# First projection's products recorded among the tokens' transposes

## The chip, the cores and the metric

The kernel runs on one core of one Trainium2 chip. The metric is the device time of one execution in microseconds; lower is better. The kernel before was run three times (1632.19, 1634.96 and 1637.48 us, median 1634.96). One further execution was recorded by the hardware profiler.

## The reference, cut to what matters

One layer of a hybrid decoder for 1024 prompt tokens and 32 sample tokens (8 sequences of 4). The part that the change touches is the first norm and the columns of the input projection that feed the state-space group:

```python
def token_mixer(h, ...):              # h = rms_norm(x, norm_g[0])
    z = h @ w_in                      # 1024 -> 512 (a) + 512 (g) + 512 (u)
    a, g, u = z[..., :512], z[..., 512:1024], z[..., 1024:]
    v = a * sigmoid(g)                # convolution group
    ...
    s, h_last = s5_layer(u, ...)      # 32 groups, 64 complex states each, scan over time
```

After that come a convolution of width 31, LayerNorm, the S5 scan, two output projections, cross-attention over 256 memory tokens, and a SwiGLU feed-forward network of width 2816. All of it is computed in fp32 accuracy.

## The kernel before

Tokens stand along the free dimension: 1056 tokens are two halves (b = 0, 1) of two parts (s) of 264 columns, 8 sample tokens and 256 prompt tokens. A feature tile is [128, 2, 264]. Every weight product is three fp32r matmuls: weight and activation are each split into a high part (ScalarE, `hi`) and a low part (VectorE or GpSimd, `lo`), and `mac` (L187) issues high x high, high x low, low x high, each for both parts s, so one feature tile of one output block costs 6 matmuls of 264 columns, and one output block of 128 columns costs 48.

The input stage loads the rows of half 0 (four DMAs of 512 KB, L126), transposes them on TensorE into 8 feature tiles (`tokens_in`, L280: per tile four 128x128 transposes and two of 8 columns), and has ScalarE copy each tile out of PSUM twice: `xf` (L290, which SyncE's queue stores to DRAM as the residual) and `hi` scaled by the norm's gain (L293). VectorE forms `lo` (L294). `tokens_rsqrt` makes the norm's factors r0 by a Newton iteration on VectorE and small matmuls with a matrix of ones. The norm's factor is applied after the product: `project_u` (L325) runs the 48 matmuls of one output block, multiplies by r0 (L81, tile `u`) and stores `u` to DRAM. Blocks j = 0, 1 are made here for both halves, from two weight tiles `wu` (L321, `st_wi`, `hi_wi`, `lo_wi`); the stage after it (`filler` and `s5_stream`) interleaves the convolution group's projections (`pg`, `pa`) with the S5 stream. That stream has 16 pairs of groups; for each two pairs `s5_matrices` has VectorE build tables (`ct`, `ebd`, `fbd`), TensorE turns them (`psS`, `psK`), `s5_states` multiplies them with `uf`, which is `u` read back from DRAM (`pw`), VectorE forms `X` and `Y`, scans (`M`), and `s5_outputs` gives `py`. In parallel with the input stage VectorE computes the S5 parameters in a long chain of operations on 16 columns, which starts from four small loads (`srow`, `ldt`, `drow`).

The order of instructions on each engine is fixed when the kernel is built: a list scheduler takes what is ready by its own timing, the highest priority first, and `high_priority(offset=...)` shifts a block's priority (a larger offset comes earlier). On the chip each engine then runs its list in order. PSUM tiles come from three pools: `mm` (two buffers), `pw` (one) and `sm` (two); `mm_tile` takes every third tile from `pw`, unless the list `streams` holds something.

[...]

Of the kernel before, what the change touches and what calls it, by code (L numbers as in the profile page):

```python
# [13 lines left out]
ALU = mybir.AluOpType  # L14
# [4 lines left out]
P = 128  # L19
D = 1024  # L20
KT = 8
NB = 8
W = 264
# [19 lines left out]
def decode_step(ctx: ExitStack, tc: tile.TileContext, I, O):  # L43
    nc = tc.nc
    act, dve, pool, pe, sync = nc.scalar, nc.vector, nc.gpsimd, nc.tensor, nc.sync
# [9 lines left out]
    def unit(name, dt=F32, shape=(P, 2, W), tag="act"):  # L55
        return acts.tile(list(shape), dt, tag=tag, bufs=BUFS[tag], name=name)

    def tmp(name, dt=F32, shape=(P, 2, W)):
        return unit(name, dt, shape, "tmp")
# [3 lines left out]
    def mm_tile(name):  # L63

        turn[0] += 1
        third = turn[0] % 3 == 0 and not streams
        return ps.tile([P, 2, 512], F32, tag="pw" if third else "mm", bufs=1 if third else 2, name=name)

    def pw_tile(name):
        return ps.tile([P, 2, 512], F32, tag="pw", bufs=1, name=name)  # L70

    streams = []

    def sm_tile(name):
        return ps.tile([P, 512], F32, tag="sm", bufs=2, name=name)

    def dscr(name, shape):
        return dram.tile(shape, F32, tag=name, name=name)

    def tt(out, a, b, op, eng=None):  # L80
        (eng or dve).tensor_tensor(out, a, b, op)  # L81
# [18 lines left out]
    def run(*gens):  # L100

        gens = [g for g in gens if g is not None]
        while gens:
            gens = [g for g in gens if next(g, END) is not END]

    END = object()
# [14 lines left out]
    def load_rows(b):  # L121
        rows.append([[startp.tile([P, D], F32, name=f"rows{b}{s}{i}") for i in range(2)] for s in range(2)])
        with tc.high_priority(offset=4000000 - 2000000 * b):
            for s in range(2):
                for i in range(2):
                    sync.dma_start(rows[b][s][i], xp[2 * b + s, i * P:(i + 1) * P])  # L126
# [57 lines left out]
    def wcols(w, n, name, eng=None):  # L184
        return wrect(w, 0, w.shape[1] // P, n * P, P, f"{name}{n}", eng)

    def mac(outs, whi, wlo, xhi, xlo, parts, first, last):  # L187

        for i, (a, b) in enumerate(((whi, xhi), (whi, xlo), (wlo, xhi))):
            for out, part in zip(outs, parts):  # L190
                pe.matmul(out, lhsT=a, rhs=part(b), start=first and i == 0, stop=last and i == 2)  # L191

    both = [lambda x: x[:, 0, :], lambda x: x[:, 1, :]]
    one = [lambda x: x]

    def dense(out, wh, wl, xs, first=True, last=True, k0=0, step=P):

        outs = [out[:, 0, :W], out[:, 1, :W]]
        for k, (xh, xl) in enumerate(xs):
            c = slice(k0 + k * step, k0 + k * step + P)  # L200
            mac(outs, wh[:, c], wl[:, c], xh, xl, both, first and k == 0, last and k == len(xs) - 1)
# [69 lines left out]
    h = [[None] * KT for _ in range(2)]  # L271
    r0 = [None, None]
# [7 lines left out]
    def tokens_in(b):  # L280
        for k in range(KT):
            c = slice(k * P, (k + 1) * P)
            pt = mm_tile(f"xt{b}{k}")
            for s in range(2):
                q = slice(32 * (2 * b + s), 32 * (2 * b + s) + 8)
                for i in range(2):
                    pe.transpose(pt[:, s, 8 + i * P:8 + (i + 1) * P], rows[b][s][i][:, c], ident)
                pe.transpose(pt[:, s, 0:8], srows[q, c], ident[q, q])
            xt = startp.tile([P, 2, W], F32, tag="xf", bufs=13, name=f"xf{b}{k}")
            act.activation(xt, pt[:, :, :W], AF.Copy)  # L290
            sync.dma_start(xres[b][k], xt)
            hi, lo = unit(f"h{b}{k}h", F32R), unit(f"h{b}{k}l", F32R)
            act.activation(hi, pt[:, :, :W], AF.Copy, scale=gain(0, k))  # L293
            dve.scalar_tensor_tensor(lo, xt, gain(0, k), hi.bitcast(F32), op0=ALU.mult, op1=ALU.subtract)  # L294
            h[b][k] = (hi, lo)
            yield

    def tokens_rsqrt(b):
        for s in range(2):
            for i in range(2):  # L300
                sum_squares(1 + 4 * b + 2 * s + i, rows[b][s][i])
        if b == 0:
            sum_squares(0, srows)
        n0, n1 = (0, 5) if b == 0 else (5, 9)
        newton(y0[:, n0:n1], ssq[:, n0:n1], D, 1e-6)
        r0[b] = rtile(f"x{b}")
        for s in range(2):
            q = slice(32 * (2 * b + s), 32 * (2 * b + s) + 8)
            o = sm_tile(f"r0{b}{s}")
            d8 = tiny.tile([104, 8], F32, tag="d8", name=f"d8{b}{s}")  # L310
            dve.tensor_scalar(d8[q], ident[q, q], y0[q, 0:1], None, op0=ALU.mult)
            pe.matmul(o[:, 0:8], lhsT=ones[q], rhs=d8[q], start=True, stop=True)
            for i in range(2):
                d = tiny.tile([P, P], F32, tag="rd", bufs=3, name=f"r0d{b}{s}{i}")
                j = 1 + 4 * b + 2 * s + i
                dve.tensor_scalar(d, ident, y0[:, j:j + 1], None, op0=ALU.mult)
                pe.matmul(o[:, 8 + i * P:8 + (i + 1) * P], lhsT=ones, rhs=d, start=True, stop=True)
            act.activation(r0[b][:, s, :], o[:, :W], AF.Copy)

    with tc.high_priority(offset=1500000):  # L320
        wu = {j: wcols(I["w_in"], 8 + j, "wi", dve if j == 0 else pool) for j in range(2)}  # L321
    load_rows(1)
    unat = [[dscr(f"u{b}_{j}", [P, 2, W]) for j in range(4)] for b in range(2)]

    def project_u(j, b, w):  # L325
        pu = mm_tile(f"pu{j}{b}")
        dense(pu, *w, h[b])
        u = tmp(f"u{j}{b}")
        tt(u, pu[:, :, :W], r0[b], ALU.mult)
        sync.dma_start(unat[b][j], u)  # L330
# [28 lines left out]
    def ahead(gen):  # L359

        while True:
            with tc.high_priority(offset=1000000):
                if next(gen, END) is END:
                    return
            yield
# [108 lines left out]
    tt(f_re, f_re, den, ALU.mult)  # L474
    tt(f_im, f_im, den, ALU.mult)
    gt = [ahead(tokens_in(b)) for b in range(2)]
    run(gt[0])
    tokens_rsqrt(0)
    for j, n in ((0, 2), (1, 3)):
        for _ in range(n):  # L480
            next(gt[1])
        project_u(j, 0, wu[j])
    pp = sm_tile("pp1")
    perm = unit("perm", F32, (4 * TAPS, 4, TAPS), "co")
    pool.memset(perm, 0.0)
# [47 lines left out]
        tt(bbar[:, o], bbar[:, o], b1, op, pool)  # L533

    run(gt[1])
    with tc.high_priority(offset=1000000):
        tokens_rsqrt(1)
    for j in range(2):
# [983 lines left out]
    for s4 in range(4):  # L1522
        b, s = s4 // 2, s4 % 2
# [44 lines left out]
```

## Time and profile before

| | |
|---|---|
| median of three runs | 1634.96 us |
| profiled execution's own time | 1629.99 us |
| its span, first to last instruction | 1628.3 us |
| TensorE busy / weight loads busy | 1501.8 us (92%) / 1454.1 us (89%) |
| VectorE, ScalarE, GpSimd busy | 1004.9 us (62%), 685.6 us (42%), 327.6 us (20%) |
| mean granted TensorE clock | 0.972 |

The table says what each engine did over the whole span. It doesn't say what set the end of the stage that is changed: that is read from the stage's own stretch of the timeline. The input stage ends where the first matmul of `pg` starts, at 69.78 us. A matmul's own duration includes its latency; the pace is the distance between starts.

### The profile page before, as it was taken

Reading aid. Unit: us, or ns where it says so; the run is one execution under the profiler, and the core shown is the slowest. Engines: PE = TensorE matmul, PEld = TensorE weight load, DVE = VectorE, ACT = ScalarE, POOL = GpSimd, SP = SyncE. Lnnn points to the kernel's source line nnn. Section 1 sums busy time; section 2 is a strip of 40 time slices with the busy share of each in tenths; the row PEclk is TensorE's granted clock in tenths of the full one; section 3 lists DMA queues with packets and bytes.
Section 4 is the critical chain, followed back from the end, with each engine's and each line's share of the span. In section 5 each row is a group of like instructions: output and inputs, shape, how many; then the busy total and the mean of one; then the engine's idle time right before and its main releaser. Section 6 shows DMA issues by size and latency. Waiting matters only on the chain. (4 is left out here: it accounts for less than half of the span.)

```text
span 1628.3 us, 29327 instructions
## 1 busy us (share of the span) xinstructions
PE 1501.8 (92%) x11731; PEld 1454.1 (89%) x11731; DVE 1004.9 (62%) x1689; ACT 685.6 (42%) x1242; POOL 327.6 (20%) x409
## 2 busy tenths in 40 slices
PE   7999889889999979878968899999999999999995
PEld 5888878889999979778968899999999999999995
DVE  6889786466468855484486877666555542444345
ACT  6444534457564544374355643333333334122122
POOL 1366566330334420051120000000000000000005
PEclk9998999999999989989989999999999999999998
DMA  8522223456244503454436643333222234232124
GB/s 232 166 73 70 65 71 101 139 155 202 78 138 152 184 14 117 143 168 140 142 118 182 218 141 124 124 119 99 80 79 79 67 113 149 89 101 69 50 66 158
DMA packets 216116, 194.33 MB, mean 119 GB/s; under 512 B 21900, under 2 KB 180036, under 8 KB 215972
## 3 DMA queue, kind: packets, MB, share of 16 engines
q1 hardware_dynamic: 215852, 192.30, 38.3%
q8 instruction: 92, 1.51, 0.4%
q14 instruction: 44, 0.36, 0.1%
q10 hardware_dynamic: 128, 0.16, 0.0%
HBM read 146.33 MB, written 46.51 MB: 118 GB/s over the span
## 5 line engine op out<-in xcount | busy, mean ns | idle before, releaser
L1497 POOL COPY ysam<-ya 128x8 f32<-128x8 f32 x32 | 5.6, 192 | 745.9 <-DVE ya L81 745.1
L81 DVE TENSOR_TENSOR ya<-ya,fd 128x528 f32<-128x528 f32 x64 | 45.1, 704 | 105.8 <-PE fd L191 105.8
L176 ACT ACTIVATE hi_wd<-st_wd 128x1024 fp32r<-128x1024 f32 x20 | 21.2, 1060 | 121.5 <-PE fd L191 121.3
L191 PE MATMUL pao<-oth,hi_wa 128*128 128x264 f32 x256 | 53.8, 292 | 14.4 <-ACT mg L979 13.3
L81 DVE TENSOR_TENSOR c<-c,X 128x528 f32<-128x528 f32 x51 | 35.9, 703 | 39.7 <-PE X L1310 39.7
L191 PEld LDWEIGHTS pao<-oth,hi_wa 128*128 128x128 f32 x256 | 40.9, 194 | 15.2 <-ACT mg L979 13.9
L191 PE MATMUL pao<-otl,hi_wa 128*128 128x264 f32 x256 | 53.7, 291 | 0.0
L191 PE MATMUL pao<-oth,lo_wa 128*128 128x264 f32 x256 | 53.2, 289 | 0.5 <-DVE lo_wa L84 0.5
L643 PE MATMUL pcv<-vf,cm 128*128 128x128 f32 x320 | 45.2, 292 | 7.2 <-ACT ob L645 4.5
L643 PEld LDWEIGHTS pcv<-vf,cm 128*128 128x128 f32 x320 | 41.9, 206 | 9.0 <-issue 5.7
L191 PEld LDWEIGHTS pao<-oth,lo_wa 128*128 128x128 f32 x256 | 40.8, 193 | 0.8 <-DVE lo_wa L84 0.7
L191 PEld LDWEIGHTS pao<-otl,hi_wa 128*128 128x128 f32 x256 | 41.0, 194 | 0.1
L84 DVE TENSOR_TENSOR lo_wa<-st_wa,hi_wa 128x1024 fp32r<-128x1024 f32 x16 | 19.4, 1214 | 34.0 <-ACT hi_wa L176 34.0
L84 DVE TENSOR_TENSOR kl<-pkr,kh 128x512 fp32r<-128x512 f32 x32 | 21.9, 690 | 28.7 <-ACT kh L89 28.5
L84 DVE TENSOR_TENSOR lo_wd<-st_wd,hi_wd 128x1024 fp32r<-128x1024 f32 x20 | 24.5, 1225 | 24.4 <-ACT hi_wd L176 21.2
L224 DVE RECIPROCAL r_n<-r_n 128x528 f32<-128x528 f32 x8 | 27.6, 3450 | 12.0 <-ACT r_n L223 12.0
L753 DVE TENSOR_TENSOR_SCAN M<-rho,X 128x256 f32<-128x256 f32 x32 | 29.8, 956 | 7.4 <-POOL X L81 7.3
L89 ACT ACTIVATE wc<-t 128x512 fp32r<-128x512 f32 x22 | 13.9, 632 | 47.2 <-PE X L1310 25.1
L89 ACT ACTIVATE kh<-pkr 128x512 fp32r<-128x512 f32 x32 | 18.9, 598 | 30.7 <-PE pkr L1135 29.5
L81 DVE TENSOR_TENSOR c<-c,c 128x528 f32<-128x528 f32 x45 | 31.6, 702 | 0.1
L645 ACT ACTIVATE ob<-pcv,cbias 128x128 f32<-128x128 f32 x32 | 11.6, 364 | 46.4 <-PE pcv L643 46.3
L1385 ACT ACTIVATE c<-Z 128x528 f32<-128x528 f32 x22 | 13.5, 612 | 41.4 <-PE Z L1310 41.4
(2047 smaller groups left out, 5720.1 us busy)
## 6 DMA issues: line engine op xcount, KB each, us to landing
hr<-hid SPq DMA_DIRECT2D x44, 264.0 KB
ww<-in_w_gate_dram SPq DMA_DIRECT2D x22, 512.0 KB
ww<-in_w_up_dram SPq DMA_DIRECT2D x22, 512.0 KB
st_wd<-in_w_down_dram SPq DMA_DIRECT2D x20, 512.0 KB
hid<-c SPq DMA_DIRECT2D x38, 264.0 KB
xo<-x SPq DMA_DIRECT2D x32, 264.0 KB
kr<-in_cache_mem_k_dram SPq DMA_DIRECT2D x32, 256.0 KB
st_wo<-in_w_out_dram SPq DMA_DIRECT2D x16, 512.0 KB
```

The costliest lines, as they stand in the source:

```text
L81: (eng or dve).tensor_tensor(out, a, b, op)
L84: eng.tensor_tensor(lo, x, hi.bitcast(F32), ALU.subtract)
L89: act.activation(hi, x, AF.Copy)
L176: act.activation(hi[:, :cols], stv, AF.Copy)
L191: pe.matmul(out, lhsT=a, rhs=part(b), start=first and i == 0, stop=last and i == 2)
L224: dve.reciprocal(r, r)
L643: pe.matmul(o, lhsT=cm[:, d].rearrange("p c t -> p (c t)"), rhs=vf[:, g, 4 - d:CH - d], start=d == 0, stop=d == 4)
L645: act.activation(ob[:, g4], o, AF.Identity, bias=cbias[:, gg:gg + 1])
L753: dve.tensor_tensor_scan(out=M[:, i], data0=rho[:, pair:pair + 1].to_broadcast([P, 256]), data1=X[:, i], initial=0.0, op0=ALU.mult, op1=AL ...
L1385: act.activation(c22, Z[:, :, :W], AF.Copy)
L1497: pool.tensor_copy(ysam[:, n, 2 * b + s, :], yacc[b][n][:, s, 0:8])
```

## The change

Three things change. The two weight tiles of the first projection get a higher priority, above the small parameter loads and the rows of half 1. A new generator `project_steps` records the first projection's products of half 0 one feature tile at a time, so that the 6 matmuls of tile k can stand between transposes; its PSUM tile comes from `pw`, and `streams` holds something until half 1 has been transposed, so that transposes have only the two `mm` buffers. Block j = 0 is recorded two tiles behind the transposes of half 0, block j = 1 among the transposes of half 1. Blocks of half 1 go through `project_u` as before.

```diff
-    with tc.high_priority(offset=1500000):
+    with tc.high_priority(offset=2500000):
         wu = {j: wcols(I["w_in"], 8 + j, "wi", dve if j == 0 else pool) for j in range(2)}
...
+    def project_steps(j, b, w):
+
+        pu = pw_tile(f"pu{j}{b}")
+        for k in range(KT):
+            c = slice(k * P, (k + 1) * P)
+            mac([pu[:, 0, :W], pu[:, 1, :W]], w[0][:, c], w[1][:, c], *h[b][k], both, k == 0, k == KT - 1)
+            yield
+        u = tmp(f"u{j}{b}")
+        tt(u, pu[:, :, :W], r0[b], ALU.mult)
+        sync.dma_start(unat[b][j], u)
...
     gt = [ahead(tokens_in(b)) for b in range(2)]
-    run(gt[0])
+    gu = [ahead(project_steps(j, 0, wu[j])) for j in range(2)]
+    streams.append(1)
+    for k in range(KT):
+        next(gt[0])
+        if k > 1:
+            next(gu[0])
+    next(gt[0], END)
     tokens_rsqrt(0)
-    for j, n in ((0, 2), (1, 3)):
-        for _ in range(n):
-            next(gt[1])
-        project_u(j, 0, wu[j])
+    run(gu[0])
+    for k in range(KT):
+        next(gt[1])
+        next(gu[1])
+    run(gu[1])
...
     run(gt[1])
+    streams.clear()
     with tc.high_priority(offset=1000000):
         tokens_rsqrt(1)
```

On SyncE's queue, at the program's start, the two weight tiles `st_wi` (512 KB each) and the small loads stand so before:

```order
L126 DMA rows_89<-in_x_prompt_dram 128x1024
L138 DMA ldt<-in_log_dt_dram 16x2
L135 DMA srow<-in_lam_im_dram 16x128
L133 DMA srow<-in_lam_re_dram 16x128
L141 DMA drow<-in_d_skip_dram 16x32
L126 DMA rows_148<-in_x_prompt_dram 128x1024
...
L126 DMA rows_151<-in_x_prompt_dram 128x1024
L173 DMA st_wi_136<-in_w_in_dram 128x8x128
L173 DMA st_wi_142<-in_w_in_dram 128x8x128
L334 DMA h0row<-in_state_ssm_re_dram 128x128
```

The weights stand at the end of this piece, just ahead of `h0row`. With the change the same piece of SyncE's queue reads:

```order
L126 DMA rows_89<-in_x_prompt_dram 128x1024
L173 DMA st_wi_136<-in_w_in_dram 128x8x128
L173 DMA st_wi_142<-in_w_in_dram 128x8x128
L135 DMA srow<-in_lam_im_dram 16x128
L138 DMA ldt<-in_log_dt_dram 16x2
L133 DMA srow<-in_lam_re_dram 16x128
L141 DMA drow<-in_d_skip_dram 16x32
L126 DMA rows_148<-in_x_prompt_dram 128x1024
...
L126 DMA rows_151<-in_x_prompt_dram 128x1024
L345 DMA h0row<-in_state_ssm_re_dram 128x128
```

The weights moved ahead of the four small loads and of half 1's rows (148 to 151); the rows of half 0 (86 to 89) stay first.

On TensorE, with the change, the list from the fourth transposed tile (`xt_385`) on begins so (`pq` are the transposes of the small loads, `pu_378` is block 0 of half 0); before, the tiles of half 0 stood here one behind the other and `pu` began ten tiles in:

```order
L384 MATMUL pq<-ident,srow 128x48
L385 MATMUL pq<-ident,drow 32x16
L191 MATMUL pu_378<-h00h,hi_wi_138 128x264 x2
L191 MATMUL pu_378<-h00l,hi_wi_138 128x264 x2
L191 MATMUL pu_378<-h00h,lo_wi_139 128x264 x2
L191 MATMUL pu_378<-h01h,hi_wi_138 128x264
L287 MATMUL xt_385<-ident,rows_86 128x128
L287 MATMUL xt_385<-ident,rows_87 128x128
L191 MATMUL pu_378<-h01h,hi_wi_138 128x264
L288 MATMUL xt_385<-ident,srows 128x8
```

What moved: after three tiles the products of tile k follow, and each further tile's transposes stand between them; `pq`, and with it the small loads, stands ahead of the first product.

On VectorE, around the multiplications `u_868` and `u_920` that close the projections of half 1, the list before is this (`ct_040` to `ct_051`, `ebd`, `fbd` are S5 tables of the first two pairs, `ct_140` of the next two, `lo_wi_971` a weight tile of the next stage):

```order
L81 TENSOR_TENSOR ebd_936<-ct_041_1033,ct_041_1034 64x2x4x16 x2
L84 TENSOR_TENSOR lo_wi_965<-st_wi_962,hi_wi_964 128x1024
...
L81 TENSOR_TENSOR ct_050_1039<-pw,cmat 128x160
...
L81 TENSOR_TENSOR fbd_937<-ct_050_1039,ct_050_1040 64x2x5x16 x2
...
L81 TENSOR_TENSOR fbd_937<-ct_051_1045,ct_051_1046 64x2x5x16 x2
L81 TENSOR_TENSOR ct_140_1255<-pwr,bbar 128x2x64
...
L84 TENSOR_TENSOR lo_wi_971<-st_wi_968,hi_wi_970 128x1024
...
L81 TENSOR_TENSOR u_868<-pu_819,r_x_796 128x528
L81 TENSOR_TENSOR u_920<-pu_871,r_x_796 128x528
L81 TENSOR_TENSOR ebd_936<-ct_140_1255,ct_140_1256 64x2x4x16 x2
```

Here all tables for the first two pairs, and `ct_140`, stand ahead of both `u`. With the change the same place on VectorE reads:

```order
L84 TENSOR_TENSOR lo_wi_965<-st_wi_962,hi_wi_964 128x1024
...
L84 TENSOR_TENSOR lo_wi_971<-st_wi_968,hi_wi_970 128x1024
L81 TENSOR_TENSOR ct_040_1028<-pwr,bbar 128x2x64
L81 TENSOR_TENSOR u_868<-pu_819,r_x_796 128x528
L81 TENSOR_TENSOR u_920<-pu_871,r_x_796 128x528
...
L81 TENSOR_TENSOR ebd_936<-ct_040_1027,ct_040_1028 64x2x4x16 x2
L81 TENSOR_TENSOR ct_041_1033<-pwr,bbar 128x2x64
...
L81 TENSOR_TENSOR ebd_936<-ct_041_1033,ct_041_1034 64x2x4x16 x2
L81 TENSOR_TENSOR ct_050_1039<-pw,cmat 128x160
...
L81 TENSOR_TENSOR fbd_937<-ct_050_1039,ct_050_1040 64x2x5x16 x2
```

The tables of the first two pairs, and the first of the next two, moved behind both `u`. From the S5 stream's sixth pair on (some 130 us into the span before) the lists of the two kernels are all but the same.

## Rows read from the trace of the kernel before

**Rows 1.** Stretches (us): span, busy by engine (instructions), granted clock, DMA share, GB/s.

```profile
13.66:28.20 14.54, 14.54 (x55) 9.32 (x55) 12.28 (x50) 10.49 (x18) 2.80 (x4) 1.00 1.01 281
...
31.40:63.80 32.40, 32.40 (x244) 29.50 (x243) 27.76 (x104) 15.28 (x29) 9.73 (x21) 1.00 0.67 208
63.80:69.78 5.98, 2.56 (x21) 1.61 (x19) 5.85 (x15) 3.75 (x9) 1.96 (x3) 0.96 0.38 111
69.78:72.60 2.82, 2.82 (x13) 2.82 (x14) 2.62 (x8) 1.37 (x5) 1.08 (x3) 0.50 0.79 241
...
79.24:108.77 29.53, 29.53 (x224) 28.04 (x224) 24.32 (x41) 13.44 (x24) 21.70 (x30) 1.00 0.19 56
```

**Rows 2.** TensorE's timeline: start, length, line, out<-in, count, idle before and its releaser.

```profile
10.35 0.90 PE L287 MATMUL xt<-ident,rows 128*128 128x128 f32 x3 [1.08 <-DMA rows<-in_x_prompt_dram]
...
28.80 0.64 PE L191 MATMUL pu<-h00l,hi_wi 128*128 128x264 f32 x2
29.24 0.64 PE L191 MATMUL pu<-h00h,lo_wi 128*128 128x264 f32 x2
...
37.44 0.41 PE L191 MATMUL pu<-h07l,hi_wi 128*128 128x264 f32 x2
37.69 0.40 PE L191 MATMUL pu<-h07h,lo_wi 128*128 128x264 f32 x2
...
43.11 0.38 PE L287 MATMUL xt<-ident,rows 128*128 128x128 f32 x2
...
44.10 0.39 PE L191 MATMUL pu<-h03h,lo_wi 128*128 128x264 f32 x1
...
69.78 0.81 PE L191 MATMUL pg<-h00h,hi_wi 128*128 128x264 f32 x2 [0.98 <-DVE u L81]
```

**Rows 3.** VectorE's timeline, the same columns.

```profile
10.69 0.22 DVE L370 COPY srow<-ldt 16x128 f32<-16x128 f32 x1 [4.30 <-DMA ldt<-in_log_dt_dram]
12.11 0.21 DVE L376 COPY lam<-pq 128x48 f32<-128x48 f32 x1 [1.20 <-PE pq L374]
...
22.81 1.23 DVE L84 TENSOR_TENSOR lo_wi<-st_wi,hi_wi 128x1024 fp32r<-128x1024 f32 x1 [2.07 <-ACT hi_wi L176]
...
28.11 0.50 DVE L404 TENSOR_SCALAR th<-th 128x16 f32<-128x16 f32 x1
...
30.18 0.76 DVE L294 SCALAR_TENSOR_TENSOR h07l<-xf,gains,h07h 128x528 fp32r<-128x528 f32 x1
...
57.36 0.28 DVE L81 TENSOR_TENSOR ebd<-ct,ct 64x128 f32<-64x128 f32 x1
...
67.27 0.49 DVE L81 TENSOR_TENSOR ct<-pwr,bbar 128x128 f32<-128x128 f32 x2
...
69.02 1.32 DVE L81 TENSOR_TENSOR u<-pu,r_x 128x528 f32<-128x528 f32 x2
```

**Rows 4.** ScalarE's timeline, the same columns.

```profile
21.72 1.06 ACT L176 ACTIVATE hi_wi<-st_wi 128x1024 fp32r<-128x1024 f32 x1 [3.43 <-DMA st_wi<-in_w_in_dram]
...
28.66 0.22 ACT L406 ACTIVATE ab<-th 128x16 f32<-128x16 f32 x1 [0.88 <-DVE th L404]
28.90 1.28 ACT L407 ACT_TABLE_LOAD   x1
...
30.58 0.60 ACT L290 ACTIVATE xf<-xt 128x528 f32<-128x528 f32 x1
31.07 0.70 ACT L293 ACTIVATE h10h<-xt,gains 128x528 fp32r<-128x528 f32 x1
```

**Rows 5.** VectorE's later timeline, the same columns.

```profile
72.72 1.10 DVE L81 TENSOR_TENSOR ct<-pw,cmat 128x160 f32<-128x160 f32 x2
...
75.82 0.49 DVE L81 TENSOR_TENSOR ct<-pwr,bbar 128x128 f32<-128x128 f32 x2
...
79.24 0.69 DVE L81 TENSOR_TENSOR X<-pw,tab 128x512 f32<-128x512 f32 x1 [1.25 <-ACT wsam L743]
...
108.77 2.30 DVE L753 TENSOR_TENSOR_SCAN M<-rho,X 128x256 f32<-128x256 f32 x2
```

## The prediction, made before the changed kernel was run

> **What bounds the kernel now.** I read the stretches first, then the timelines of the three engines in that stage. Over its whole span TensorE is 92% busy, but the input stage is not like the rest, and the stretches show three parts of it [rows 1]. From 13.66 to 28.20 TensorE is busy without a gap, with transposes; from 31.40 to 63.80 it is busy without a gap, with products; from 63.80 to 69.78 it is busy for 2.56 of 5.98 us while VectorE is busy for 5.85. So the stage is bound by TensorE first and by VectorE at its end: `pg`, which opens the next stage at 69.78, waits for `u` [rows 2], which VectorE made at 69.02 behind S5 tables [rows 3].
>
> The pace of TensorE is the second thing to see. Two products start 0.44 us apart at 28.80 and 0.25 us apart at 37.44 [rows 2]: 0.22 and 0.122 us each for 264 columns. The stretch from 69.78 to 72.60 has a granted clock of 0.50, which is 1.2 GHz. The column says 1.00 for 13.66 to 28.20, but since the products at 28.80 have the pace of 1.2 GHz I take that stretch for 1.2 GHz too: there 55 matmuls of transposes and factors took 14.54 us, 0.264 each, so a tile of six costs 1.59 us, against 0.99 for one between products (43.11 to 44.10) [rows 1, 2]. TensorE thus spent some 14 us on transposes at half pace, busy all the time, and the clock did not rise.
>
> **Part by part.** My sum goes along the new order, with durations of the profiled execution.
>
> *Loads.* The last rows of half 0 landed at 10.35 [rows 2]. The first weight tile was ready at 21.72 [rows 4], and between them 2 MB of rows and 1 MB of weights landed: 3.1 MB in 11.4 us, 0.27 MB per us. With the weights right behind half 0's rows, 1.05 MB takes 3.9 us: 14.2. The small loads now stand behind them: `ldt`, which VectorE got at 10.69 [rows 3], comes at about 14.5, 3.8 us later; at best it is not held up (10.7), at worst the queue delays it another 2 us. Half 1's rows then land by 22, and the order uses them only after six tiles of products, past 25, so they cost nothing. This is the price of the change: the S5 parameter chain starts 3.8 us late, and so does the first product, since `pq` stands ahead of it in TensorE's list. `lam` moves from 12.11 to 15.9, the first product to 15.5.
>
> *First projection.* TensorE has to run 48 products, 7 tiles and the factors' ten small matmuls: 48 x 0.122 + 7 x 0.99 + 1.3 = 14.1 us at full pace. `pg` ran 2.8 us slowly before the clock rose [rows 1], which costs 1.4: the block would end at 15.5 + 14.1 + 1.4 = 31.0. But the eighth tile is held by something else. ScalarE's list has `ab`, a table load and two sines ahead of it, and `ab` waits for VectorE's `th` [rows 4]. VectorE took 16.0 us from `lam` to `th` (12.11 to 28.11), of which 2.07 was a wait for weights that now come early, and 1.8 is work that now stands ahead of `lam`: the weight's low part, 1.1, and the first tile's, 0.7 like the eighth's [rows 3]. That leaves 12.1 us, so `th` comes at 28.0. Then `ab`, the table and the sines (2.1), the eighth tile's two copies (1.1) [rows 4], its low part (0.7) and four products (0.5): the block ends at 32.5. Before, it ended at 37.9 [rows 2]. Gain here 5.4 us, of which TensorE could have had 6.9. The small parameter tables (`wrow`, `prow`), whose transposes now stand near the block's end, have 0.5 MB less of stored tiles ahead of them; I cost them at nothing, up to 1.5 us.
>
> *The rest of the projections.* TensorE needed 25.8 us from there to the end of the last product at 63.8, without a gap [rows 1, 2]. The same work remains. Three tiles of half 1 now stand in a row with two PSUM buffers, where ScalarE needs 1.1 us for one against 0.99: with some waiting 1.2 us. It ends at 59.5, and `u` is made by 60.5. Can VectorE follow? The eighth low part was done by 30.9, and from 31.40 VectorE had 27.8 us of work to 63.80 and 5.2 more to 69.02 [rows 1, 3]. Nine rows of S5 tables, from 57.36 to 67.27, 7.4 us in all, go behind `u` [rows 3]. So 25.6 us from 32.0, where the eighth low part is done now: 57.6, about 2 us of slack. Both `u` end at 60.5 instead of 70.3: 9.8 us earlier. `pg` starts at about 59.5.
>
> *What is given back.* The tables did not vanish. Behind `u` VectorE now has the 7.4 us, and 3.4 more that stood there before and still has to come ahead of the first `X` (two tables, a `sg`, two small ones); the first `X` comes 10.8 us behind `u`, at 71.3. The other path to it, `u` stored and read back, took 9.0 us (70.3 to 79.24) and would give 69.5, so VectorE decides. Gain 7.9. From `X` to the scan of the fourth pair at 108.77 VectorE worked 24.3 us in 29.5 [rows 1, 5]. Five rows of tables, 72.72 to 75.82, 3.45 us [rows 5], now lie in this stretch. They can fill its 5.2 us of waiting wholly (27.8 us) or not at all (33.0), and one more activation table load, 1.28 us [rows 4], may fall on the chain. I take half of the waiting as filled: 30.4 us, the scan at 101.7, a gain of 7.1. Then the lists are the same, and all engines are shifted alike.
>
> Sum: 4.3 (the products end at 59.5, not 63.8) + 5.5 (`u` follows them after 1.0 us instead of 6.5) - 1.9 - 0.8 = 7.1 us. The profiled execution took 1629.99 and would take 1622.9. It lies 5 us under the median of the runs, 1634.96; I take the difference off that: **1628**.
>
> [...]
>
> **The rivals.**
>
> *The clock stays at 1.2 GHz through the first projection* (slower). The order puts 1.59 us of transposes beside each 1.32 us of products. For it: transposes alone did not raise the clock in 14 us [rows 1]. Against it: where tiles stood between products at 43.11 the pace stayed full [rows 2], though there the clock was already up. Price: 48 x 0.22 + 7 x 1.59 + 2.6 = 24.3, so the block ends at 39.8, later than before; three more tiles and the small transposes at half pace cost 2.8, and the clock rises only in block 1, for another 1.6. The products end at 71.2, `u` at 72.2, the first `X` 10.8 later at 83.0, which is 3.8 later than before, and the scan loses another 0.9: 4.7 us slower, 1640. It decides if products still start 0.44 us per two beyond some 25 us.
>
> *The S5 stream eats the gain.* The tables fill no waiting, the table load falls on the chain, and `X` is 1 us later: 33.0 + 1.3 from 72.3 puts the scan at 106.6, a gain of 2: 1633. For it: VectorE waited there for GpSimd and ScalarE in short pieces that a table of 0.5 to 1 us overfills. Against: the tables are independent work, and lie exactly between waits.
>
> *More than forecast.* The eighth tile is not held up by `th`, the read-back decides `X` (69.5 less 1.5), the tables fill all waiting: the scan at 68.0 + 27.8 = 95.8 to 2 us later, a gain of 11 to 13: 1623. For it: at 31.0 TensorE alone would allow it. Against: `lam` can hardly come earlier.
>
> **Chances.** Forecast (gain of 5 to 9) 0.45; eaten gain (0 to 5) 0.25; more 0.12; slow clock 0.18. A change of 0.3%, 4.9 us, is about what a measurement tells from none. Faster takes the forecast, the larger gain, and loses a little at the forecast's lower end: 0.55. The slow clock at 1640 lies on the bound, and two thirds of it count as slower: 0.12. The rest is 0.33. The range reaches from the larger gain (1622) to the slow clock (1640), each with 1 to 2 us for the scatter of the runs, 1632 to 1637 before: 1620 to 1641; the forecast's own is 1625 to 1631.
>
> **What would show it.** Right: `hi_wi` near 14 us, `lam` near 16; products 0.25 us per two before 25 us; block 0's last product near 32.5; `pg` near 59.5 with hardly a wait; the first `X` near 71, the fourth scan near 102. Wrong: products at 0.44 past 25 us, VectorE not ready for `u` at 60, `X` waiting for something other than VectorE, or a shift at the fourth scan that is gone by the end of the S5 stream.

## The result, and the profile after

The changed kernel takes 1646.34 us (median of 8 runs, 1639.07 to 1651.55); the kernel before, run beside it, took 1635.22 (median of 8, 1627.42 to 1638.61). The ratio is 1.0074, 95% interval 1.0049 to 1.0098: slower by 11 us, where 1628 was predicted and 1641 was the upper end of the range. The profiled execution took 1639.07, span 1637.4, and was the fastest of the eight; a second one further down lies near the median. One run below (1671.00 us, of the changed kernel with plain products) fell into a slower state and is left out of its median and ratio.

First the stretches of the changed kernel, with the columns of [rows 1]: the first projection at half pace, then from VectorE's eighth low part to `u`, from `u` to the first `X`, and on to the fourth pair's scan.

```profile
15.15:34.20 19.05, 19.05 (x76) 15.40 (x75) 14.79 (x75) 10.18 (x20) 3.81 (x7) 1.00 0.88 221
35.87:70.09 34.22, 34.22 (x258) 31.15 (x258) 28.44 (x97) 18.85 (x35) 12.99 (x23) 1.00 0.59 183
70.09:81.72 11.63, 10.65 (x82) 9.49 (x81) 10.70 (x28) 5.32 (x12) 3.75 (x5) 1.00 0.40 114
81.72:112.72 31.00, 27.29 (x186) 25.59 (x186) 29.41 (x51) 14.39 (x25) 19.90 (x29) 0.89 0.18 52
```

TensorE's timeline after, with the columns of [rows 2]:

```profile
15.15 0.81 PE L191 MATMUL pu<-h00h,hi_wi 128*128 128x264 f32 x2
15.76 0.64 PE L191 MATMUL pu<-h00l,hi_wi 128*128 128x264 f32 x2
16.20 0.64 PE L191 MATMUL pu<-h00h,lo_wi 128*128 128x264 f32 x2
...
31.38 0.64 PE L191 MATMUL pu<-h04h,lo_wi 128*128 128x264 f32 x2
31.82 0.42 PE L191 MATMUL pu<-h05h,hi_wi 128*128 128x264 f32 x1
...
34.49 0.40 PE L191 MATMUL pu<-h05h,lo_wi 128*128 128x264 f32 x2
34.73 0.28 PE L191 MATMUL pu<-h06h,hi_wi 128*128 128x264 f32 x1
...
38.78 0.41 PE L191 MATMUL pu<-h07h,lo_wi 128*128 128x264 f32 x2
...
66.11 0.40 PE L191 MATMUL pg<-h00h,hi_wi 128*128 128x264 f32 x2
```

The products start 13 us earlier than before, and then run at half pace for 19 us: 0.44 us for two at 15.76 and still at 31.38, 0.24 from 34.49 on. The prediction and the expectations call this pace 1.2 GHz, an estimate from the starts: 264 columns in 0.22 us are 1.2 columns per ns, as at 70.38 before, where the granted clock reads 0.50. Before, the pace doubled within some 3 us [rows 1, 2]. TensorE is busy for all 19.05 us, with 76 instructions. So block 0 ends at 39.0, later than the 37.9 of before, although it began at 15.15. `pg` starts at 66.11 and waits for nothing.

VectorE's timeline after answers to [rows 3, 5]:

```profile
14.47 0.22 DVE L381 COPY srow<-ldt 16x128 f32<-16x128 f32 x1 [0.71 <-DMA ldt<-in_log_dt_dram]
15.86 0.20 DVE L387 COPY lam<-pq 128x48 f32<-128x48 f32 x1
...
29.41 0.17 DVE L415 TENSOR_SCALAR th<-th 128x16 f32<-128x16 f32 x1
31.69 0.77 DVE L294 SCALAR_TENSOR_TENSOR h06l<-xf,gains,h06h 128x528 fp32r<-128x528 f32 x1 [1.80 <-ACT h06h L293]
35.18 0.77 DVE L294 SCALAR_TENSOR_TENSOR h07l<-xf,gains,h07h 128x528 fp32r<-128x528 f32 x1 [0.83 <-ACT h07h L293]
...
64.79 2.16 DVE L694 TENSOR_SCALAR turn<-turn 128x256 f32<-128x256 f32 x1
...
70.09 1.31 DVE L81 TENSOR_TENSOR u<-pu,r_x 128x528 f32<-128x528 f32 x2
...
81.72 0.69 DVE L81 TENSOR_TENSOR X<-pw,tab 128x512 f32<-128x512 f32 x1
...
112.72 2.28 DVE L772 TENSOR_TENSOR_SCAN M<-rho,X 128x256 f32<-128x256 f32 x2
```

VectorE ran its list in order: the waits of 1.80 and 0.83 us for `h06h` and `h07h` in these rows held up the S5 tables behind the low parts. Both `u` of half 1 come at 70.09 (69.02 before), 4 us after TensorE's last product; the first `X` at 81.72 is 2.5 us later than before, the scan at 112.72 is 4.0 later. At the S5 stream's last scan it is 4.2 (268.9 against 264.7), at the first score product 9.3 (569.75 against 560.43), and there it stays.

### The profile page after: what moved, and what is told of

It is laid out like the page before. It is cut to its first block, busy times and chain, and to the rows that moved or that the text cites. A ratio compares the mean times of both kernels' runs of the same rounds, so it can differ in the third digit from the quotient of the medians.

```text
span 1637.4 us, 29319 instructions
## 1 busy us (share of the span) xinstructions
PE 1508.8 (92%) x11731; PEld 1461.4 (89%) x11731; DVE 1009.0 (62%) x1689; ACT 687.5 (42%) x1243; POOL 326.7 (20%) x409
## 5 line engine op out<-in xcount | busy, mean ns | idle before, releaser
L662 PEld LDWEIGHTS pcv<-vf,cm 128*128 128x128 f32 x320 | 42.6, 209 | 10.0 <-issue 5.8
L191 PE MATMUL pov<-pt,vm 128*128 128x256 f32 x192 | 29.5, 296 | 4.2 <-ACT pt L89 2.4
L191 PE MATMUL sc<-km,q 128*128 128x256 f32 x192 | 27.8, 301 | 5.1 <-DVE mx L1056 5.1
L664 ACT ACTIVATE ob<-pcv,cbias 128x128 f32<-128x128 f32 x32 | 11.6, 364 | 48.8 <-PE pcv L662 43.4
```

The lines of the kernel that those rows point to most:

```text
L662: pe.matmul(o, lhsT=cm[:, d].rearrange("p c t -> p (c t)"), rhs=vf[:, g, 4 - d:CH - d], start=d == 0, stop=d == 4)
L664: act.activation(ob[:, g4], o, AF.Identity, bias=cbias[:, gg:gg + 1])
```

## The experiments

My theory: six products between two tiles are too few to bring TensorE to full pace, 0.25 us per two, and that made the projection late. The rival: the S5 parameters, 3.8 us later, made the loss through VectorE whatever the clock does.

**Priority alone.**

```
-    with tc.high_priority(offset=1500000):
+    with tc.high_priority(offset=2500000):
         wu = {j: wcols(I["w_in"], 8 + j, "wi", dve if j == 0 else pool) for j in range(2)}
```

> The kernel before with only the priority of the first weights raised; the products stay recorded in a row behind the tiles. Theory (products thinned out by transposes kept TensorE at 1.2 GHz from 15 to 34 us, and that is where the input stage lost): here the products stand close together from about 28 us, so two of them start 0.25 us apart by 32 us, block 0 ends by 38.5, the first X by 81, and the time is 1633 to 1639, at least 7 us under the changed kernel. Rival (the S5 parameters, which come 3.8 us later behind the weights, make the loss through VectorE): lam near 15.9, th near 30, first X near 82, and 1643 to 1647 as in the changed kernel.

Measured: 1639.15, ratio 1.0041 [1.0021, 1.0062]. The products in TensorE's timeline of this run:

```profile
29.46 0.79 PE L191 MATMUL pu<-h00h,hi_wi 128*128 128x264 f32 x2
30.04 0.64 PE L191 MATMUL pu<-h00l,hi_wi 128*128 128x264 f32 x2
...
36.09 0.41 PE L191 MATMUL pu<-h03h,hi_wi 128*128 128x264 f32 x2
36.34 0.40 PE L191 MATMUL pu<-h03l,hi_wi 128*128 128x264 f32 x2
```

In a row the products brought the clock up (a transpose pair at 33.88 is already fast, 0.38 us to the next start where the one at 33.12 took 0.56), though at 34, not 32. `lam` was at 15.35, yet the first `X` came at 79.23, where it was before: late parameters alone did not move it. The 1639 was 0.15 over my range, so about half of the change's loss appears without its products, and it arises later: at the fourth scan this execution was 2.8 us behind before's (111.55 against 108.77), at the last 3.7.

**Interleaving alone.** In the changed kernel:

```
-    with tc.high_priority(offset=2500000):
+    with tc.high_priority(offset=1500000):
         wu = {j: wcols(I["w_in"], 8 + j, "wi", dve if j == 0 else pool) for j in range(2)}
```

> The changed kernel with the weights' priority put back, so that rows and small loads go first and the weights land near 21.5 us. Theory (thinned products keep the clock at 1.2 GHz): only three tiles of half 0 are left to thin the products, which start near 22.5; they are at 0.44 us per two until the last tile is through, about 30, and block 0 ends at 36 to 38.5; pg near 66, first X 79 to 81, time 1634 to 1641. Rival (late parameters): lam is back at 12.1 and nothing is lost, 1632 to 1636, with the first X no later than 79.2.

Measured: 1635.17, ratio 1.0022 [1.0008, 1.0036]; first product 22.44, 0.44 per two to 29.54 and 0.24 from 31.62, `pg` 66.5, `X` 80.79. The pace and `X` are as the theory had them, though block 0 ended at 39.3, past its 38.5; the time lies in both ranges. `lam` at 11.75 did not bring `X` back.

**Small loads first.** In the changed kernel, and likewise for `srow[16:32]`, `ldt` and `drow`:

```
-    with tc.high_priority(offset=2000000):
+    with tc.high_priority(offset=3000000):
         sync.dma_start(srow[0:16], I["lam_re"].rearrange("o (a g) n -> (o a) (g n)", g=2))
```

> The changed kernel with ldt, srow and drow issued ahead of the weights; products thinned as before. Theory (clock): lam is back near 12, but products still start 0.44 us per two until about 33, block 0 ends at 38 to 40, pg near 66, the first X within 1.5 us of the 81.7 of the changed kernel, and 1642 to 1647. Rival (late parameters): X comes 3 us earlier, at 78.5, and the time falls to 1635 to 1640.

Measured: 1648.01, ratio 1.0111 [1.0090, 1.0132]. `lam` at 11.57, but `X` at 85.94: the rival is out, and my theory's size was too small. Block 0's end and block 1's start in TensorE's timeline of this run:

```profile
43.93 0.64 PE L191 MATMUL pu<-h07l,hi_wi 128*128 128x264 f32 x2
44.37 0.64 PE L191 MATMUL pu<-h07h,lo_wi 128*128 128x264 f32 x2
49.08 0.51 PE L191 MATMUL pu<-h00h,hi_wi 128*128 128x264 f32 x2
```

Block 0 ran at half pace to its end at 44.8. VectorE, with its parameters early, does those first and the tiles' low parts later (`h01l` at 19.32, in the changed kernel at 16.36).

**Clock raised first.**

```
+    wm = startp.tile([P, W], F32R, name="wm")
+    dve.memset(wm.bitcast(F32), 1.0)
+    def warm(n, l, r):
+        t = sm_tile("warm")
+        with tc.high_priority(offset=6000000):
+            for _ in range(n):
+                pe.matmul(t[:, :W], lhsT=l, rhs=r, start=True, stop=True)
+    warm(48, wm[:, :P], wm)
+    warm(8, ones, rows[0][1][0][:, :W])
```

> The changed kernel with 56 products of constants and of tokens, whose result nobody reads, ahead of and between the first tiles, while TensorE waits for loads. Theory (clock), if the mixture of products and transposes holds the clock once it is up: products of block 0 start 0.25 us per two from 16 us on, block 0 ends at 31 to 34, pg at 59 to 62, the first X at 72 to 76, and 1629 to 1637. If the mixture lets the clock fall: 0.44 per two again from some point between 18 and 25 us, block 0 ends at 37 to 40 and 1643 to 1648. Rival (late parameters, VectorE): the clock changes TensorE's pace but not the first X, which stays within 1 us of 81.7, and 1643 to 1648.

Measured: 1647.53, ratio 1.0099 [1.0077, 1.0121]. Stretches of this run, then rows of its TensorE timeline:

```profile
9.66:13.22 3.56, 3.56 (x18) 3.00 (x17) 0.00 (x0) 2.05 (x5) 0.00 (x0) 1.00 1.21 261
16.20:33.00 16.80, 15.77 (x61) 12.53 (x62) 12.20 (x54) 7.16 (x13) 3.10 (x7) 0.51 0.87 222
34.00:40.00 6.00, 6.00 (x42) 4.78 (x42) 2.91 (x16) 5.18 (x10) 0.00 (x0) 1.00 1.00 326
```

```profile
17.23 0.59 PE L202 MATMUL pu<-h00h,hi_wi 128*128 128x264 f32 x1 [1.67 <-ACT h00h L304]
...
27.65 0.64 PE L202 MATMUL pu<-h01h,lo_wi 128*128 128x264 f32 x2
```

The clock was up ahead of the mixture (four transposes took 0.59 us from 13.83 on; before, two took 0.62 at 13.66) and fell just before it began, in a wait of 1.67 us for ScalarE; it was granted 0.51 for 16.8 us, in which TensorE was busy for 15.77. Here the mixture did not bring it back before 33 us. The run isn't clean: its extra products also put `lam` at 18.36 (15.86 in the changed kernel), and `X` came at 88.48, far outside the rival's 81.7.

**Products doubled.**

```
             mac([pu[:, 0, :W], pu[:, 1, :W]], w[0][:, c], w[1][:, c], *h[b][k], both, k == 0, k == KT - 1)
+            if j == 0 and k < KT - 1:
+                t = sm_tile(f"more{k}")
+                for i in range(6):
+                    pe.matmul(t[:, :W], lhsT=w[0][:, c], rhs=h[b][k][0][:, i % 2, :], start=True, stop=True)
```

> The changed kernel with 42 more products into a scratch bank beside the first projection's first seven steps: twelve products stand between two tiles instead of six, nothing else is changed and nobody reads the extra ones. Theory (too few products among the transposes keep the clock at 1.2 GHz): with twice the products the clock rises, two products 0.25 us apart by 22 us instead of 34, and although TensorE has 42 products more, block 0 ends at 34 to 38 against 39.0, with th, X and the time no later than in the changed kernel: first X 77 to 82, 1638 to 1647. Rival (any transposes between products hold the clock down until they end): 0.44 per two until beyond 34 us, block 0 ends 9 us later, at 46 to 49, first X at 88 or later, and 1650 to 1658.

Measured: 1636.39, ratio 1.0025 [1.0012, 1.0037]: 8 us less than the changed kernel by the two ratios (10 by the medians), with 42 products more. TensorE's timeline of this run:

```profile
16.25 1.52 PE L334 MATMUL more<-h00h,hi_wi 128*128 128x264 f32 x6
...
19.55 1.00 PE L334 MATMUL more<-h01h,hi_wi 128*128 128x264 f32 x6
20.39 0.41 PE L191 MATMUL pu<-h01l,hi_wi 128*128 128x264 f32 x2
20.64 0.41 PE L191 MATMUL pu<-h01h,lo_wi 128*128 128x264 f32 x2
```

The six extra products take 1.52 us at 16.25 and 1.00 at 19.55: the clock is up by 20 us and stays, block 0 ends at 36.5, and the time is below my range. One thing was added in the source, on the engine that was thought to have too much to do, and the time falls. But the list scheduler also put other work elsewhere. VectorE's timeline of this run:

```profile
70.86 1.05 DVE L81 TENSOR_TENSOR ct<-pwr,bbar 128x128 f32<-128x128 f32 x2
71.84 1.31 DVE L81 TENSOR_TENSOR u<-pu,r_x 128x528 f32<-128x528 f32 x2
...
79.83 0.69 DVE L81 TENSOR_TENSOR X<-pw,tab 128x512 f32<-128x512 f32 x1
```

Ahead of `u` of half 1 stand 18 instructions that make S5 tables (`ct`, `ebd`, `fbd`), as in the kernel before; in the changed kernel there are 2. So `pg` starts at 64.71, 1.4 us earlier than in the changed kernel, `u` comes 1.75 later (VectorE is busy for 7.04 of the 7.13 us between them), and `X` 1.9 earlier, since it follows 8.0 us behind `u` instead of 11.6. The run shows that the clock rose by 20 us with twelve products between tiles and that this kernel is faster. How much of the 8 us came through the clock and how much through the other order on VectorE it does not show. Its profiled execution ended only 1.3 us ahead of the changed kernel's first, and 7.4 ahead of the second further down.

**Small loads first, products in a row.** In the kernel before (the second edit for all four small loads):

```
-    with tc.high_priority(offset=1500000):
+    with tc.high_priority(offset=2500000):
         wu = {j: wcols(I["w_in"], 8 + j, "wi", dve if j == 0 else pool) for j in range(2)}
...
-    with tc.high_priority(offset=2000000):
+    with tc.high_priority(offset=3000000):
         sync.dma_start(srow[0:16], I["lam_re"].rearrange("o (a g) n -> (o a) (g n)", g=2))
```

> The kernel before, products in a row, with the small loads ahead of the weights and the weights ahead of half 1's rows: against the run with the weights' priority alone (1639.15, ratio 1.0041) only the small loads move. Theory A (what that run lost, it lost by lam coming 3.2 us later): lam back at 12, th by 27, first X at 78 to 80, and 1631 to 1636. Rival B (half 1's rows and tables behind the weights, or the order of the later work, cost it): first X within 1 us of 80.5 and 1637 to 1642.

Measured: 1635.95, ratio 1.0019 [1.0005, 1.0033]; `lam` 11.93, `X` 80.28. The time is on A's side, `X` on B's; with priority alone `X` was even at 79.23, so the parameters' arrival doesn't set it. Still, with the products in a row early parameters may be worth some 3 us (ratio 1.0041 to 1.0019, with intervals that overlap). In the executions profiled they tell behind the first `X`: the fourth scan follows it 29.5 us later here, and 32.3 with priority alone.

**Each kernel a second time** (no edit).

> The kernel before, profiled a second time: how far one execution differs from another behind the input stage. If the drift of about 5 us between 300 and 560 us belongs to the changed order, this execution has its first states' product (pso) within 0.5 us of 274.0, the score stage (sc) within 2 us of 560.4, and half-clock stretches of 93 us in all, give or take 5. If such drifts come by chance of the clock's stretches, pso to sc differs by 3 us or more from the 286.4 of the first execution.

> The changed kernel, profiled a second time. Same question: products at 0.44 us per two until 34 us again (within 1.5 us), pg near 66, first X at 81.7 within 0.7; pso to sc within 2 us of the 291.5 of its first execution if the drift belongs to the order, 3 us or more off if it comes by chance.

Measured: before 1630.31, changed 1645.20. The changed kernel's second execution is not its first over again. Its stretches, then rows of its TensorE timeline:

```profile
14.97:21.80 6.83, 5.50 (x27) 4.45 (x26) 6.81 (x22) 5.00 (x8) 4.04 (x7) 1.00 1.02 335
21.80:42.30 20.50, 20.35 (x79) 16.43 (x80) 12.38 (x71) 8.43 (x16) 0.00 (x0) 0.51 0.82 202
```

```profile
18.93 0.40 PE L191 MATMUL pu<-h01h,lo_wi 128*128 128x264 f32 x2
...
21.95 0.70 PE L191 MATMUL pu<-h02l,hi_wi 128*128 128x264 f32 x2 [1.48 <-DVE h02l L294]
...
42.18 0.59 PE L191 MATMUL pu<-h07h,lo_wi 128*128 128x264 f32 x2
```

and of its VectorE timeline:

```profile
73.66 1.31 DVE L81 TENSOR_TENSOR u<-pu,r_x 128x528 f32<-128x528 f32 x2
...
85.28 0.69 DVE L81 TENSOR_TENSOR X<-pw,tab 128x512 f32<-128x512 f32 x1
```

The clock rose at 18.5, 3.5 us after the first product, much as I had predicted; at that pace TensorE ran out of low parts and waited 1.48 us; then the clock fell and the stretch from 21.80 reads 0.51 for 20.5 us. `pg` came at 69.68, `X` at 85.28, 6.0 later than before. With the same order, the time at which the clock is up for good varies by 8 us. This pair is the cleanest test of the clock, since every engine's list is the same in both executions: block 0 ended 3.6 us later than in the first (42.6 against 39.0), `u` came 3.6 later, `X` 3.6, the fourth scan 3.5, and the whole 6.1. In this pair, what delays the first block arrives at the fourth scan in full. Behind the stage the two kernels do keep their own drift: from `pso` to the first score product 286.4 and 287.6 us before, 291.5 and 291.8 after.

**Transposes as plain products**, in the changed kernel and in the one before.

```
-                    pe.transpose(pt[:, s, 8 + i * P:8 + (i + 1) * P], rows[b][s][i][:, c], ident)
+                    pe.matmul(pt[:, s, 8 + i * P:8 + (i + 1) * P], lhsT=rows[b][s][i][:, c], rhs=ident, start=True, stop=True)
-                pe.transpose(pt[:, s, 0:8], srows[q, c], ident[q, q])
+                pe.matmul(pt[:, s, 0:8], lhsT=srows[q, c], rhs=ident[q, q], start=True, stop=True)
```

> The changed kernel with each of the tokens' transposes written as a plain product with the identity: same operands, same shapes, same places in the order. Theory (transposes don't raise the clock and thin out what does): now everything TensorE does there counts, the clock rises by 21 us, two products of the first projection start 0.25 us apart from there on, block 0 ends at 30 to 35, pg at 58 to 64; what then decides is VectorE, so the first X comes at 76 to 80.5, and the time is 1631 to 1638. Rival (the clock follows how fast TensorE is kept supplied, not what kind of instruction it runs): 0.44 until 33 us or later, block 0 ends at 38 or later, X at 81.5 or later, 1641 to 1649.

> The kernel before with the same replacement: the tokens' transposes as plain products with the identity. Theory: half 0's eight tiles, 14.5 us at half pace before, raise the clock themselves by about 16 us; the tiles are through by 25 and the first product starts there instead of 28.2, at 0.25 us per two from the first on; block 0 ends at 31 to 36, pg at 66 to 70 since VectorE is not done with its tables sooner, first X 76 to 79.5, 1628 to 1634, at best 3 us under the kernel before. Rival: no change of pace, first product at 28 at 0.44 per two, 1632 to 1636.

Measured: 1654.74, ratio 1.0134 [1.0109, 1.0158], and 1651.78, ratio 1.0131 [1.0113, 1.0148]. Both expectations fell. A stretch of the first run, from its first product on:

```profile
16.75:58.00 41.25, 41.25 (x160) 36.31 (x160) 21.71 (x116) 12.81 (x23) 3.73 (x7) 1.00 0.57 157
```

A stretch of the second run, and rows of its TensorE timeline there and behind it:

```profile
14.64:40.60 25.96, 25.96 (x96) 22.23 (x97) 14.66 (x62) 12.01 (x20) 4.10 (x7) 1.00 0.91 244
```

```profile
14.64 1.22 PE L287 MATMUL xt<-ident,rows 128*128 128x128 f32 x4
15.79 0.59 PE L288 MATMUL xt<-ident,srows 8*128 8x8 f32 x2
...
41.21 0.64 PE L191 MATMUL pu<-h00l,hi_wi 128*128 128x264 f32 x2
...
45.54 0.28 PE L191 MATMUL pu<-h03h,lo_wi 128*128 128x264 f32 x1
```

Each plain f32 product went out as two instructions (four for the two of a half tile at 14.64), so a half tile takes 1.67 us (14.64 to 16.31) and a tile 3.35, twice the 1.64 of a transposed one (13.66 to 15.30 before; the prediction's 1.59 is an average with the factors' matmuls). And TensorE, busy without a gap from 14.64 to 40.60, is still at 0.44 per two at 41.21; 4.9 us of products in a row brought it up by 45.54. In the first run, where products stand between these tiles, TensorE was busy without a gap for 41.25 us and the last two products of block 0, at 57.24, still took 0.44 us to the next start. So it isn't the transposing alone: the tokens' tiles in f32 didn't raise the clock in either form, and the projection's products in a row did. Whether their type or their size makes the difference was not tried.

**Doubled, small loads first.**

> The run with doubled products with ldt, srow and drow issued ahead of the weights as well. There the clock was up by 20 us and yet the first X came at 79.8, because VectorE made u only at 71.8, 7 us behind the last product. Theory (with the clock up VectorE's chain from lam decides, and the late parameters count): lam at 12 instead of 15.9, u of half 1 at 67 to 70, first X at 76 to 78.5, 1630 to 1634. Rival (VectorE waits there for tiles and PSUM, not for its own earlier work): first X within 1 us of 79.8, 1635 to 1638.

Measured: 1640.10, ratio 1.0059 [1.0042, 1.0075]. `lam` 11.94, but two products were 0.25 us apart only from 24 us on, not from 20, `u` came at 74.24, `X` at 83.73. Neither side had it: with its parameters early, VectorE again made the tiles' low parts later.

**Both column blocks beside the tiles**, without and with the small loads first. The tiles of half 0 go to the buffer `pw`, the products to the two `mm` buffers:

```
-            pt = mm_tile(f"xt{b}{k}")
+            pt = (mm_tile if b else pw_tile)(f"xt{b}{k}")
...
-        pu = pw_tile(f"pu{j}{b}")
+        pu = mm_tile(f"pu{j}{b}")
...
         if k > 1:
             next(gu[0])
+            next(gu[1])
...
-    run(gu[0])
-    for k in range(KT):
-        next(gt[1])
-        next(gu[1])
-    run(gu[1])
+    run(gu[0], gu[1])
+    streams.clear()
...
     run(gt[1])
-    streams.clear()
```

> The changed kernel with both column blocks of the first projection of half 0 recorded beside its tiles, so twelve needed products stand between two tiles; the tiles use the one PSUM buffer that the products had, the products the other two. Theory (products must be dense among the transposes for the clock to rise): 0.25 us per two by 22 us, u of both blocks of half 0 made by 42 to 46 (38.5 and 48.6 before), last product at 57 to 62 against 63.8. If VectorE can follow, as the prediction had it: u of half 1 at 60 to 65, first X at 71 to 76, 1624 to 1631. If VectorE is the bound (u of half 1 at 67 or later in spite of that): first X at 77 to 81, 1631 to 1638.

> The same with ldt, srow and drow ahead of the weights. If VectorE's start decides (lam at 12 instead of 15.9): first X 2 to 4 us earlier than with both columns alone, and the time lower by as much. If its waits for tiles and low parts decide, as the doubled run with small loads first suggests, where the clock rose later: clock up at 24 to 30 us instead of 20 to 22, first X within 1 us or up to 3 us later.

Measured: 1645.09, ratio 1.0077 [1.0058, 1.0097], and 1644.55, ratio 1.0083 [1.0060, 1.0106]; `X` at 84.11 and 84.30. Stretches of the first, the one without:

```profile
24.30:45.30 21.00, 20.17 (x142) 17.18 (x141) 14.85 (x84) 10.99 (x23) 0.00 (x0) 1.00 0.68 202
45.30:51.40 6.10, 4.14 (x25) 2.54 (x23) 5.78 (x28) 6.10 (x13) 1.42 (x3) 1.00 0.44 172
51.40:61.00 9.60, 9.12 (x38) 6.81 (x37) 8.81 (x22) 6.03 (x11) 3.82 (x6) 0.52 0.46 175
```

Twelve needed products a tile had the clock up by 25 us (two took 0.44 us to the next start at 22.83, four are over in 0.74 at 27.45), later than I expected, and both `u` of half 0 are made by 47.4. But half 1's eight tiles now have no product beside them: TensorE waits for ScalarE's copies (4.14 of 6.10 us busy, ScalarE all 6.10), the clock is down again from 52 us on, and the last product ends at 72.0. Both of my ranges missed (1624 to 1638 in all), and so did the 57 to 62 for the last product. The loss moved from half 0's tiles to half 1's. No version that was run beats the kernel before.

## Why the prediction was wrong, step by step

*Loads and starts: right.* `hi_wi` at 13.34 (near 14), `ldt` 14.47 (14.5), `lam` 15.86 (15.9), first product 15.15 (15.5), `th` 29.41 (28.0).

*The step that failed* is in the first projection: "`pg` ran 2.8 us slowly before the clock rose [rows 1], which costs 1.4: the block would end at 15.5 + 14.1 + 1.4 = 31.0", and with `th` 32.5. I took the rise from a stretch where products stood alone. Among the tiles the products stayed at 0.44 us per two to 34.1 in one execution, and in the other the clock rose for 3.3 us and was down again to 42.3; block 0 ended at 39.0 and 42.6. So the products ended at 66.1 instead of 59.5, 6.6 us late. That this lateness reaches the scan is shown by the pair of executions with one order; the doubled run agrees, with 8 to 10 us that came back, but part of that may be its other order on VectorE. Late parameters are not the main cause: among the tiles early ones did not help (1648.01, and 1640.10 doubled). With the products in a row they may be worth some 3 us, so a share of the loss may be theirs.

The first rival had the mechanism and the block's end, 39.8 (39.0). Its other sizes came near partly by luck: its last product at 71.2 was 5 too late, and it had VectorE only 1.0 us behind, where it was 5.3 behind; the two errors cancel in `u` (72.2, made by 71.4), `X` (83.0, 81.7) and the 4.7 lost at the scan (4.0). Its 1640 counts from the median of the runs. Counted from before's profiled execution it is 1634.7, and the changed kernel's took 1639.07: the 5 us lost behind the last scan are not in it. Why the median lies another 7 above is not shown. I gave this rival 0.18. What I held against it, full pace around the tiles at 43.11 [rows 2], was a clock that was up already, and [rows 1] had 14.5 us of busy transposes that didn't raise it: the sum needed a price for the mixture, and I had none from this trace. The run with plain products had the same tiles for 26 us without a transpose, and behind them two products still took 0.44 us to the next start (41.21).

*"About 2 us of slack" for VectorE: wrong as well.* From the eighth low part to `u` I had 25.6 us of work; it took 34.2, with 28.4 busy [the stretch 35.87 to 70.09]. It also began 3.9 us late, at 35.87 instead of 32.0, behind the slow eighth tile. Together, 3.9 late, 2.8 more work and 5.8 idle, that turns 57.6 into 70.09, so `u` was made 5.3 us behind the last product and not 1.0. How much of the 5.8 idle is the slow tiles' doing was not measured. Some of the added work is length: `turn` took 2.16 us, 0.28 at 63.51 before, and GpSimd was busy for 2.00 of those 2.16; whether that made it longer was not tested. Even with the clock up, in the doubled run, `u` came at 71.84 and not at 60.5, though there with the tables ahead of it again. What VectorE would need with the clock up, the forecast's order and no extra products stays open: the run with both column blocks, made to tell it, lost its clock later.

*`X` 10.8 us behind the end of `u`: right* (10.3 in both executions, 71.40 to 81.72 in the first). It could only hand on a late `u`. The way to the fourth scan was right too (31.0 for 30.4). So the 11.0 us by which that scan missed 101.7 are 6.6 of products, 4.3 of VectorE, -0.5 and 0.6.

*"Then all engines are shifted alike": wrong.* From the last scan to the score stage the same 2186 matmuls took 4 to 5 us longer in both executions; the rows are one execution of before, then one after:

```profile
264.67:560.43 295.76, 276.78 (x2186) 269.29 (x2185) 188.85 (x271) 159.16 (x251) 104.87 (x87) 0.98 0.48 146
```

```profile
268.90:569.75 300.85, 279.24 (x2186) 271.74 (x2185) 189.31 (x271) 158.93 (x251) 103.46 (x87) 0.97 0.47 144
```

The trace's record of the granted clock has 10.2 us at the half level there before and 17.1 after. In the eleven experiments with another order this stretch took 297.5 to 303.4, longer than in both executions of before. That goes part of the way with the clock (most of them had 13.7 or 17.1), but not always: one had 6.8 and took 298.1. Nor are the lists quite alike there: between 304 and 454 us six of TensorE's matmuls, two of VectorE's instructions and four of ScalarE's stand in another place, and some 1.5 of the 5 us arise between 300 and 330. (Behind 575 us some 350 of TensorE's stand elsewhere; no time was lost there.) Why a changed start costs there is not settled.

*The account:* in the first execution 2.5 us up to `X`, 1.7 to the last scan, 5.1 to the score stage, -0.2 behind it: 9.1. In the second, near the median: 6.0, 3.3, 5.3 and 0.5: 15.2. Both are counted from before's profiled execution (1629.99), which was 5 us under its own median.

## What to carry to other kernels

Before products are put among work that fills TensorE without raising its clock, find in the trace what the pace of just that mixture is, at the program's start as well; if no row shows it, price the half pace too (here 0.44 us per two for 19 us). Putting independent work into a busy stretch can gain nothing when the stretch is busy because it is slow: here the products in a row were what raised the clock for the tiles after them (0.99 us a tile at 43.11 before, 1.64 at 13.66). Where engines work in order, follow the late tile through every queue: here VectorE lost another 4.3 us behind the products. And where a scheduler orders the instructions, compare the lists of a run that adds one thing before the difference is put down to that thing.

## What the runs showed of the hardware that was not expected

- More work took less time: 42 products more among the tiles, 1636.4 us instead of 1646.3, with VectorE's tables in another order too.
- The granted-clock column reads 1.00 up to the first change on record: 15.15 to 34.20 reads 1.00 with products at 0.44 per two, the same mixture reads 0.51 where a fall is on record ahead of it (21.80 to 42.30 of the second execution). In that first stretch the products' spacing was the measure.
- A raised clock did not last: 3.3 us at full pace, a wait of 1.48 for a low part, then 20.5 us at half; in the run with the clock raised first it fell in a wait of 1.67. That the waits caused it was not tested.
- The plain f32 products with the identity went out as two instructions each, and 26 us, nearly all of them, without a gap, left TensorE at 0.44 us per two. With the projection's products between such tiles it was busy for 41.25 us without a gap at the same pace.
